# Moving an encoder layer's SBUF tiles: one pool for each kind of tile, and one residue for all that TensorE reads

## Chip, cores, metric

The kernel runs on one core of one Trainium2 chip. The metric is the device time of one execution in microseconds, as the median of several runs.

## What is computed

One layer of an encoder trunk on 2048 tokens of width 1024, all in float32: adaptive scale, shift and gate from a conditioning vector `c`, a stick-breaking attention with 16 heads, and a SwiGLU feed-forward (width 2816), each between two RMS norms. Cut to what matters:

```python
def stick_breaking_mixer(h, w_qkv, w_o):
    ...
    for q0 in range(0, s, SB_BLOCK):                 # 128 queries at a time
        z = einsum('bthd,bshd->bhts', q[:, q0:end], k[:, :end]) * scale
        mask = s_pos < t_pos
        sp = where(mask, softplus(z), 0.0)
        rest = cumsum(sp, axis=3, reverse=True)
        a = exp(where(mask, z - rest, -inf))
        outs.append(einsum('bhts,bshd->bthd', a, v[:, :end]))
    return concatenate(outs, axis=1).reshape(b, s, D_MODEL) @ w_o

def swiglu_ffn(h, w_in, w_out):
    g, u = split(h @ w_in, 2, axis=-1)
    return (silu(g) * u) @ w_out

h = modulate(rms_norm(x, norm_g[i, 0]), sh_m, sc_m)
x = x + gt_m * rms_norm(stick_breaking_mixer(h, ...), norm_g[i, 1])
h = modulate(rms_norm(x, norm_g[i, 2]), sh_f, sc_f)
x = x + gt_f * rms_norm(swiglu_ffn(h, ...), norm_g[i, 3])
```

## The kernel before

A float32 product is made of three passes in the fp32r format: each operand is split into a rounded high part (ScalarE) and the remainder (VectorE or GpSimd), and `mm3` (L146 to L150) multiplies high by high (L148), high by low (L149) and low by high (L150). Nearly all matmuls have a moving operand of 128 x 512 and a stationary one of 128 x 128; every one brings its own weight load (PEld in the profile).

The order of work is written out by hand and fixed for all engines but SyncE, which issues the DMAs. Four stages follow one another.

- **Attention** (to about 1430 us). Eight pairs of heads, four blocks of 512 tokens. Projections (`pj`, moving `ht`, stationary `w`) run in threes between the slots of the attention: in a slot, two matmuls make the scores (`z`, L507: moving `kt`, stationary `qt`), ScalarE takes two sigmoids, VectorE a running product (`tensor_tensor_scan`, L536 and L541), GpSimd a product (L548), TensorE turns the result by matmuls with the identity (`t`, L558: the identity is the moving operand, the turned tile `a` the stationary one; 2176 of them), ScalarE and VectorE split it (`aT`), and two matmuls weigh the values (`o`, L586: moving `aT`, stationary `v`). Another 384 transposes turn the input, the values and the second norm's rows, 128 each.
- **Output projection** (`y`: moving `wo`, stationary `ohl`), to about 1580 us: 32 tiles of 24 matmuls.
- **First FFN product** (`s`: moving `r`, stationary `l`), to about 2444 us, by a scheme with seven products in the place of eight. 44 column groups of 84 matmuls each: products 1, 5, 6, 3, 7, 2, 4, four blocks of the contraction in each, three passes in each block. The right factors `r` stay in SBUF over 22 groups, in buffers of the kinds that `RIGHT_TAGS` names: `kt` for the first 9 matmuls of a group, then `v` for 9, `qt` for 18, `kt` for 12, `v` for 12, `whl` for 24. The left factors `l` are in `ht` buffers.
- **Second FFN product** (`o` of `b`, `ol`), to the end: 56 steps of 33 matmuls, moving `b` (in `kt` and `v` buffers, seven in turn of each), stationary `ol_qt` for the first 24 matmuls of a step (`qt` buffers) and `ol_aT` for the last 9 (`aT` buffers).

SBUF tiles are named by a tag, and each tag has a fixed number of buffers (`BUFS`, L51). Before, all tags lie in one pool, `att` (L153), which sets them down in the order in which they first appear, small tiles among large ones. In the built program this gives the following places (byte address in a partition, and the address modulo 512, which the parts of a tile share, since they start at multiples of 512):

| kind | bytes x buffers | address before | modulo 512 | address after | modulo 512 |
|---|---|---|---|---|---|
| identity (in `begin`) | 512 | 2,688 | 128 | 3,136 | 64 |
| `qt` | 8192 x 3 | 4,160 | 64 | 45,632 | 64 |
| `v` | 4096 x 7 | 28,736 | 64 | 70,208 | 64 |
| `wraw`, `qkn` | 4096 x 2 each | 57,408, 65,600 | 64 | 176,704, 184,896 | 64 |
| `ht` | 8192 x 5 | 73,792 | 64 | 4,672 | 64 |
| `a` | 2048 x 10 | 114,752 | 64 | 201,280 | 64 |
| `w` (scan results) | 2052 x 3 | 135,232 | 64, 96, 128 | 221,760 | 64, 96, 128 |
| `kt` | 4096 x 7 | 141,472 | 160 | 98,880 | 64 |
| `whl` | 8192 x 4 | 170,752 | 256 | 127,552 | 64 |
| `tmp` | 2048 x 4 | 203,520 | 256 | 193,088 | 64 |
| `aT` | 4096 x 4 | 211,712 | 256 | 160,320 | 64 |
| single columns | 4 to 32 | 170,144 and 228,096 | many | 228,000 | many |

Of the kernel before, what the change touches and what calls it, by code (L numbers as in the profile page):

```python
# [9 lines left out]
F32 = mybir.dt.float32  # L10
# [6 lines left out]
P = 128  # L17
# [61 lines left out]
    return ap.bitcast(F32)  # L79


@with_exitstack
def hybrid_trunk_kernel(
    ctx: ExitStack,
# [14 lines left out]
    nc = tc.nc  # L99

    const = ctx.enter_context(tc.tile_pool(name="const", bufs=1))
    dram = ctx.enter_context(tc.tile_pool(name="dram", bufs=1, space=DRAM))


    begin = const.tile([P, BT + 1], F32, name="begin")
    nc.gpsimd.memset(begin, 0.0)
    ident = begin[:, BT - P : BT]
# [42 lines left out]
        nc.tensor.matmul(acc, lhs[1], rhs[0], start=False, stop=last, **kw)  # L150


    att = ctx.enter_context(tc.tile_pool(name="att", bufs=2))  # L153
    zps = ctx.enter_context(tc.tile_pool(name="zps", bufs=3, space=PSUM))
    tps = ctx.enter_context(tc.tile_pool(name="tps", bufs=2, space=PSUM))
    accps = ctx.enter_context(tc.tile_pool(name="accps", bufs=3, space=PSUM))
# [1224 lines left out]
    for n, (s, f) in enumerate(groups):  # L1381
# [3 lines left out]
        for at, product in enumerate(PRODUCTS):  # L1385
            acc = banks_of[{1: 0, 6: 0, 7: 0, 4: 0, 5: 1, 3: 1, 2: 2}[product]]
            for k in range(H4):
# [18 lines left out]
                if s == 0 and 4 <= f < 4 + 2 * H4:  # L1406
                    kt, second = divmod(f - 4, 2)
# [177 lines left out]
```

## Time and profile before

| | us |
|---|---|
| median of 3 runs | 2883.05 |
| lowest, highest | 2881.68, 2887.14 |
| span of the profiled execution, its own time | 2881.7 |

The span runs from the first to the last instruction, and equals the fastest of the three runs to a tenth. Times in the profile are counted from its start. A matmul's recorded duration (some 390 ns for 512 columns) overlaps those of its neighbours, since matmuls are pipelined: the pace is the distance from one start to the next. The lines themselves stand with the prediction.

### The profile page before, as it was taken

How to read it: one execution, taken by the hardware profiler on the slowest of the kernel's cores; microseconds unless marked ns; L12 is line 12 of the kernel's file. 1: busy time of each engine (PE TensorE's matmuls, PEld its weight loads, DVE VectorE, ACT ScalarE, POOL GpSimd, SP SyncE). 2: the span in 40 equal slices, each digit the busy share in tenths (PEclk: the TensorE clock that was granted, in tenths of full speed). 3: DMA queues.
4: the chain of work that ended last, by engine and by line, in shares of the span. 5: the costliest groups of instructions: out<-in, count | busy, mean ns of one | idle time of the engine just before them, and what ended most of it. 6: DMA issues, size and time to landing. Idle time of an engine off the chain costs nothing.

```text
span 2881.7 us, 41790 instructions
## 1 busy us (share of the span) xinstructions
PE 2836.6 (98%) x13848; PEld 2337.5 (81%) x13848; DVE 2029.2 (70%) x2823; ACT 1630.5 (57%) x3263; POOL 1280.0 (44%) x2032
## 2 busy tenths in 40 slices
PE   8999999999999999999999999999999999999998
PEld 6788888888888888887888788888778888888887
DVE  6788888888888888889866766555775555133477
ACT  4787777787777877778645533334433334322343
POOL 1475666566576655657310122222122222544454
PEclk9999999999999999999999999999999999999999
DMA  8764546656665644555388544334363234544565
GB/s 313 279 207 166 187 155 222 208 178 221 196 213 174 214 125 161 190 158 200 119 286 317 170 147 153 106 110 165 110 193 106 93 110 161 190 141 149 176 220 184
DMA packets 239368, 516.84 MB, mean 179 GB/s; under 512 B 22320, under 2 KB 110384, under 8 KB 221488
## 3 DMA queue, kind: packets, MB, share of 16 engines
q1 hardware_dynamic: 239152, 514.18, 54.1%
q8 instruction: 109, 1.79, 0.2%
q14 instruction: 107, 0.88, 0.1%
HBM read 346.85 MB, written 118.49 MB: 161 GB/s over the span
## 4 chain that ended last, share of the span: by engine, by line
PE 91%; DVE 4%; DMA 2%; ACT 2%; issue 1%; POOL 0%; SPq 0%; DVEq 0%; POOLq 0%; ACTq 0%
PE s L148 9%; PE s L149 9%; PE s L150 9%; PE o L586 8%; PE z L507 8%; PE t L558 8%; PE pj L148 6%; PE pj L150 6%; PE pj L149 6%; PE o L149 5%; PE o L150 5%; PE o L148 5%; PE y L148 2%; PE y L150 2%; PE y L149 2%
## 5 line engine op out<-in xcount | busy, mean ns | idle before, releaser
L548 POOL TENSOR_TENSOR a<-a,w 128x512 f32<-128x512 f32 (+3 forms) x640 | 619.7, 968 | 221.4 <-DVE w L541 127.8
L541 DVE TENSOR_TENSOR_SCAN w<-z,c,begin 128x512 f32<-128x512 f32 x384 | 489.7, 1279 | 87.2 <-ACT z L526 66.9
L148 PE MATMUL s<-r,l 128*128 128x512 f32 x1232 | 486.1, 395 | 3.0 <-DVE p L1348 3.0
L149 PE MATMUL s<-r,l 128*128 128x512 f32 x1232 | 484.3, 393 | 0.0
L150 PE MATMUL s<-r,l 128*128 128x512 f32 x1232 | 483.7, 393 | 0.0
L524 ACT ACTIVATE a<-z 128x512 f32<-128x512 f32 (+3 forms) x640 | 346.9, 542 | 172.1 <-PE z L507 135.2
L586 PE MATMUL o<-aT,v 128*128 128x512 f32 (+3 forms) x1280 | 387.3, 384 | 0.1
L574 DVE TENSOR_TENSOR aT<-t,aT 128x512 fp32r<-128x512 f32 (+3 forms) x640 | 359.3, 595 | 23.1 <-ACT aT L568 22.6
L507 PE MATMUL z<-kt,qt 128*128 128x512 f32 (+3 forms) x1280 | 364.8, 366 | 0.0
L568 ACT CAST aT<-t 128x512 fp32r<-128x512 f32 (+3 forms) x640 | 313.9, 533 | 74.9 <-PE t L558 64.5
L526 ACT ACTIVATE z<-z 128x512 f32<-128x512 f32 (+3 forms) x640 | 345.5, 540 | 0.0
L1356 POOL TENSOR_TENSOR one<-p,p 128x512 f32<-128x512 f32 x44 | 71.2, 1617 | 590.5 <-issue 326.8
L148 PE MATMUL pj<-ht,w 128*128 128x512 f32 x768 | 312.5, 407 | 5.7 <-DVE qn L411 1.4
L149 PE MATMUL pj<-ht,w 128*128 128x512 f32 x768 | 304.2, 396 | 1.1 <-DVE ht L321 0.5
L150 PE MATMUL pj<-ht,w 128*128 128x512 f32 x768 | 304.5, 397 | 0.0
L558 PEld LDWEIGHTS t<-begin,a 128*128 128x128 f32 x2176 | 255.6, 141 | 58.8 <-DVE aT L574 10.9
L558 PE MATMUL t<-begin,a 128*128 128x128 f32 x2176 | 294.7, 273 | 8.5 <-DVE aT L574 7.4
L148 PEld LDWEIGHTS s<-r,l 128*128 128x128 f32 x1232 | 231.2, 188 | 58.5 <-ACT l L1209 2.3
L150 PEld LDWEIGHTS s<-r,l 128*128 128x128 f32 x1232 | 231.1, 188 | 53.8
L149 PEld LDWEIGHTS s<-r,l 128*128 128x128 f32 x1232 | 231.1, 188 | 53.3 <-issue 0.5
L507 PEld LDWEIGHTS z<-kt,qt 128*128 128x128 f32 x1280 | 230.2, 188 | 40.2 <-DVE w L536 0.2
L536 DVE TENSOR_TENSOR_SCAN w<-z,begin 128x128 f32<-128x128 f32 (+3 forms) x256 | 208.7, 818 | 75.6 <-ACT z L526 64.3
(158 smaller groups left out, 4879.7 us busy)
## 6 DMA issues: line engine op xcount, KB each, us to landing
ht<-h_s SPq DMA_DIRECT2D x108, 1024.0 KB, 8.1
wi<-in_win SPq DMA_DIRECT2D x86, 512.0 KB, 4.0
qt<-qn SPq DMA_DIRECT2D x124, 256.0 KB, 4.8
ol_qt<-act_s SPq DMA_DIRECT2D x56, 512.0 KB, 3.6
act_s<-S SPq DMA_DIRECT2D x66, 256.0 KB, 4.1
br<-in_wout SPq DMA_DIRECT2D x66, 256.0 KB, 3.5
h_s<-ht SPq DMA_DIRECT2D x16, 1024.0 KB, 8.0
o_s<-os SPq DMA_DIRECT2D x128, 128.0 KB, 2.6
```

What stands on the lines that cost most here:

```text
L148: nc.tensor.matmul(acc, lhs[0], rhs[0], start=first, stop=False, **kw)
L149: nc.tensor.matmul(acc, lhs[0], rhs[1], start=False, stop=False, **kw)
L150: nc.tensor.matmul(acc, lhs[1], rhs[0], start=False, stop=last, **kw)
L507: nc.tensor.matmul(z[:, :n], q[:, e, part, r * P : (r + 1) * P], k[:, e, :n], start=part == 0, stop=part == 1,)
L524: nc.scalar.activation(a[:, :n], z[:, :n], AF.Sigmoid, scale=QK_SCALE)
L526: nc.scalar.activation(z[:, :n], z[:, :n], AF.Sigmoid, scale=-QK_SCALE)
L541: nc.vector.tensor_tensor_scan(rest[:, rev], left[:, rev], begin[:, :BT][:, rev], initial=carries[r], op0=ALU.mult, op1=ALU.bypass,)
L548: nc.gpsimd.tensor_tensor(a[:, :n], a[:, :n], rest[:, 1 : n + 1], op=ALU.mult)
L558: nc.tensor.transpose(pt[:, rb * P : (rb + 1) * P], weighed[i, rb][:, j * P : (j + 1) * P], ident)
L568: nc.scalar.copy(hl[:, 0, t0:], pt[:, t0:])
L574: nc.vector.tensor_tensor(hl[:, 1, t0:], pt[:, t0:], f32(hl[:, 0, t0:]), op=ALU.subtract)
L586: nc.tensor.matmul(acc[:, t0:], lhs, hl[:, part, t0:], start=sc == qb and j == 0 and part == 0, stop=sc == 0 and j == 3 and part == 1,)
```

## The change

The one pool `att` is replaced by an object with the same `tile` method that has a pool of its own for each large kind, opened in the order of `PLACES`, and a last pool `rest` for all others: the three `w` buffers, and all single columns. Two fillers shift what follows: `lead`, 448 bytes ahead of `begin`, brings the identity to residue 64, and `gap_ht`, 64 bytes ahead of `ht`, brings all large kinds there (their sizes are multiples of 512). Each filler is set to zero once by VectorE. Sizes, buffer counts, tags and all other code stay as they are. In the built program every engine has the same instructions in the same order on the same tiles, with the same waits, but for the two added `memset`s on VectorE; the table above has the addresses.

```diff
+PLACES = [("ht", 64), ("qt", 0), ("v", 0), ("kt", 0), ("whl", 0), ("aT", 0), ("wraw", 0), ("qkn", 0), ("tmp", 0), ("a", 0)]
+
+
+class Places:
+
+    def __init__(self, ctx, tc):
+        self.of = {}
+        for tag, gap in PLACES:
+            if gap:
+                pool = ctx.enter_context(tc.tile_pool(name=f"gap_{tag}", bufs=1))
+                self.of[f"gap_{tag}"] = pool
+                tc.nc.vector.memset(pool.tile([P, gap // 4], F32, name=f"gap_{tag}"), 0.0)
+            self.of[tag] = ctx.enter_context(tc.tile_pool(name=f"at_{tag}", bufs=1))
+        self.rest = ctx.enter_context(tc.tile_pool(name="rest", bufs=1))
+
+    def tile(self, shape, dtype, name, tag, bufs):
+        return self.of.get(tag, self.rest).tile(shape, dtype, name=name, tag=tag, bufs=bufs)
...
+    lead = const.tile([P, 112], F32, name="lead")
+    nc.vector.memset(lead, 0.0)
     begin = const.tile([P, BT + 1], F32, name="begin")
...
-    att = ctx.enter_context(tc.tile_pool(name="att", bufs=2))
+    att = Places(ctx, tc)
```

## The prediction

> **What bounds the kernel now.** I read the page first: busy shares, granted clock, and the chain that ended last.
>
> ```profile
> span 2881.7 us, 41790 instructions
> PE 2836.6 (98%) x13848; PEld 2337.5 (81%) x13848; DVE 2029.2 (70%) x2823; ACT 1630.5 (57%) x3263; POOL 1280.0 (44%) x2032
> ...
> PEclk9999999999999999999999999999999999999999
> ...
> PE 91%; DVE 4%; DMA 2%; ACT 2%; issue 1%; POOL 0%; SPq 0%; DVEq 0%; POOLq 0%; ACTq 0%
> ```
>
> TensorE is the bound: 98% busy, 91% of the chain, at full clock. So I asked whether that holds in each stage (table by stage: stretch, its length, busy us of PE, PEld, DVE, ACT, POOL, then clock, DMA share, GB/s).
>
> ```profile
> 700.00:1000.00 300.00, 295.71 (x1627) 249.43 (x1626) 257.07 (x340) 234.59 (x495) 195.54 (x392) 1.00 0.60 193
> 1430.00:1580.00 150.00, 148.87 (x692) 120.80 (x691) 101.43 (x209) 75.59 (x171) 16.02 (x25) 1.00 0.86 303
> 2010.00:2444.00 434.00, 431.72 (x1863) 349.08 (x1862) 277.00 (x368) 160.77 (x287) 107.32 (x69) 1.00 0.41 132
> 2444.00:2870.00 426.00, 426.00 (x1840) 345.36 (x1839) 191.22 (x268) 143.72 (x248) 212.81 (x131) 1.00 0.55 177
> ```
>
> The longest line of TensorE's waits (total us, times, longest):
>
> ```profile
> PE t L558 <- DVE aT L574: 7.4, 14, 1.2
> ```
>
> From 1430 us on (output projection, both FFN products) TensorE has no wait to speak of, and VectorE is at about two thirds or less. In the attention VectorE stands at 257 of 300 us, 86%, behind TensorE's 296; the longest of TensorE's waits is 7.4 us in all. So what matters is how long one matmul takes, and the change touches only where its operands lie: each engine gets the same instructions in the same order, with the same waits, but for two small memsets on VectorE. Buffer counts stay too, so no transfer starts under another condition.
>
> **Does the place set a matmul's pace? The trace already has the comparison.** Matmuls are pipelined, so their pace is the distance from start to start. One column group of the first FFN product is 84 matmuls, in this order of the moving tile's place (residue modulo 512, from the table of places): 9 at 160 (kt), 27 at 64 (v, then qt), 12 at 160 (kt), 12 at 64 (v), 24 at 256 (whl). The stationary tile (ht) is at 64 throughout. The timeline of one group, TensorE alone; I keep the rows at which the place changes, and the one at which the pace settles (columns: start, duration):
>
> ```profile
> 1701.78 0.39 PE L148 MATMUL s<-r,l 128*128 128x512 f32 x1
> ...
> 1703.88 0.39 PE L148 MATMUL s<-r,l 128*128 128x512 f32 x1
> ...
> 1705.27 0.39 PE L148 MATMUL s<-r,l 128*128 128x512 f32 x1
> ...
> 1710.03 0.40 PE L148 MATMUL s<-r,l 128*128 128x512 f32 x1
> ...
> 1712.84 0.40 PE L148 MATMUL s<-r,l 128*128 128x512 f32 x1
> ...
> 1714.92 0.39 PE L148 MATMUL s<-r,l 128*128 128x512 f32 x1
> ...
> 1715.60 0.39 PE L148 MATMUL s<-r,l 128*128 128x512 f32 x1
> ...
> 1721.20 0.39 PE L148 MATMUL s<-r,l 128*128 128x512 f32 x1
> ```
>
> Differences over counts: kt, (1703.88-1701.78)/9 = 233 ns; v, the first 6, 1.39/6 = 232; then v and qt, 4.76/21 = **227**; kt, 2.81/12 = 234; v, the first 9, 2.08/9 = 231; the last 3, 0.68/3 = 227; whl, 5.60/24 = **233**. So with moving and stationary tile both at 64 the pace settles at 227 ns, after six to nine matmuls in which an earlier change of place is still felt; with the moving tile elsewhere it stays at 233 to 234. The second FFN product, with other tiles and other code, shows the same: v with qt, kt with qt, then kt with aT, which is at 256:
>
> ```profile
> 2600.15 0.39 PE L148 MATMUL o<-b,ol_qt 128*128 128x512 f32 x1
> ...
> 2601.51 0.40 PE L148 MATMUL o<-b,ol_qt 128*128 128x512 f32 x1
> ...
> 2602.92 0.39 PE L148 MATMUL o<-b,ol_aT 128*128 128x512 f32 x1
> ...
> 2605.02 0.39 PE L148 MATMUL o<-b,ol_qt 128*128 128x512 f32 x1
> ```
>
> 1.36/6 = 227 ns with both at 64, 1.41/6 = 235, 2.10/9 = 233. The Trainium skill speaks against the change here. "SBUF — State Buffer", under "Who interferes with whom", says that PE never waits on anyone, and "TensorE: Matmul & The Clock Gate", under "Step-by-step", that loading the next weights takes no read bandwidth from the running matmul; by these the change gives nothing. The trace differs by 6 ns a matmul. I go by the trace, and keep the rule as a rival.
>
> **The sum.** After the change every operand named above, and the identity of the transposes, is at 64, so I take 227 ns (226.7 from 4.76/21) for each 512-column matmul.
> - First FFN product: a group takes 1721.20-1701.78 = 19.42 us now and 84 x 0.2267 = 19.04 then: 0.38 us, in 44 groups **16.7 us**.
> - Second FFN product, 56 steps of 33 matmuls:
>
> ```profile
> L148 PE MATMUL o<-b,ol_qt x448: 387/392/399, 2444.2 to 2869.7; 128*128 128x512 f32 x150
> ...
> L150 PE MATMUL o<-b,ol_aT x168: 388/393/400, 2450.3 to 2872.3; 128*128 128x512 f32 x168
> ```
>
> From 2444.2 to 2872.3 it is 1847 distances, 428.1 us, 231.8 ns each; at 226.7 they are 418.7 us: **9.4 us**.
> - In the stages with transposes between, distances are mixed, so I use the recorded duration, which moves with them: 389 ns in the settled stretch above (1705.2 to 1710.0 us), 394 in the last 24 of the group (1715.55 to 1721.15). Groups by form in those two stretches (busy us, mean ns):
>
> ```profile
> L148 PE MATMUL s<-r,l 128*128 128x512 f32 x7 | 2.7, 389 | 0.0
> ...
> L148 PE MATMUL s<-r,l 128*128 128x512 f32 x8 | 3.2, 394 | 0.0
> ```
>
> The other products by line (minimum/median/maximum ns):
>
> ```profile
> L149 PE MATMUL y<-wo,ohl x256: 387/394/400, 1346.2 to 1579.9; 128*128 128x512 f32 x128
> ...
> L149 PE MATMUL pj<-ht,w x768: 387/394/796, 21.6 to 1336.0; 128*128 128x512 f32 x192
> ```
>
> And by form over the whole run:
>
> ```profile
> L507 PE MATMUL z<-kt,qt 128*128 128x512 f32 x896 | 283.6, 397 | 0.0
> ...
> L586 PE MATMUL o<-aT,v 128*128 128x512 f32 x896 | 301.9, 418 | 0.1
> ```
>
> Output projection: 3 lines x 256 x 5 ns = **3.8 us**. Attention: projections 3 x 768 x 5 = 11.5; scores 896 x 6 = 5.4 (397 is a mean with some waits in it, so I count 6 of the 8); weighted values 896 x 5 = 4.5 (the 418 has the start-up after the transposes in it, which I leave). That is 21.4 us if TensorE alone decides there. VectorE at 86% and waits of a few us say that it mostly does; where a slot waits on a scan, the gain turns into a longer wait. I take three quarters: **16 us**, between 0 and 21.
> - The 2176 transposes, and 384 like them:
>
> ```profile
> L558 PEld LDWEIGHTS t<-begin,a x2176: 137/141/146, 106.1 to 1417.9; 128*128 128x128 f32 x198
> L558 PE MATMUL t<-begin,a x2176: 270/272/332, 106.3 to 1418.0; 128*128 128x128 f32 x198
> ```
>
> and eight of them in the timeline:
>
> ```profile
> 299.95 1.03 PE L558 MATMUL t<-begin,a 128*128 128x128 f32 x8
> ```
>
> They take 1.03 us, the last one's 272 ns included: (1030-272)/7 = 108 ns each, identity at 128, turned tile at 64. No row shows both at 64. By the matmul rows it should not be slower; I count nothing, with 2 ns either way for the range, 5 us in all.
> - The other engines' operands move as well. ScalarE's rounding of the left factor reads from 256 in one form (ls) and from 64 in the other (wi), and takes the same:
>
> ```profile
> L1209 ACT CAST l<-ls 128x512 fp32r<-128x512 f32 x172 | 106.1, 618 | 6.5 <-DVE ls L1192 6.5
> ...
> L1209 ACT CAST l<-wi 128x512 fp32r<-128x512 f32 x129 | 79.0, 613 | 35.3 <-ACT l L1209 32.6 <-issue 1.7 <-PE s L150 0.9
> ```
>
> So nothing there. If a faster TensorE frees buffers 1.6% sooner, DMA at 41 to 60% in the long stages has room.
> - The two memsets run at the head of VectorE's queue, before the first sums:
>
> ```profile
> 0.84 0.17 DVE L110 MEMSET ones<- 128x128 f32 x1 [0.84 <-PEq L1572]
> ...
> 6.42 0.49 DVE L627 TENSOR_SCALAR asum<-ac,c_act 128x512 f32<-128x512 f32 x1 [5.34 <-DMA ac<-in_ada_first]
> ```
>
> They are smaller than the 0.17 us one, so under 0.35 us together; queued behind them are two memsets and the sums, and those wait 5.34 us for the first weights anyway. Without that cover they would cost 0.35 us once.
>
> 16.7 + 9.4 + 3.8 + 16 = 46 us. The profiled execution took its span of 2881.7 us, the fastest of the three runs (2881.68); the median, 2883.05, is 1.4 above. I forecast the median: 2883 - 46 = **2837 us**; this case's own range is 2824 (all 21 us of the attention, 5 from the transposes, and some 3 from start-ups after transposes) to 2846.
>
> **Rivals.**
> *The attention does not settle.* There the runs of equal matmuls are short: three of a projection, two of a score, then transposes. The FFN needed six to nine matmuls to settle after a change of place; if a change of form does the same, the attention keeps its 394 ns and the gain is 16.7 + 9.4 + 3.8 = 30: 2853 us. Against: the minimum in those groups is 387 already, with places mixed. Chance 0.08.
>
> *It is the height in memory, not the residue.* Every slow tile (kt, whl, aT) lies above 141,000 bytes before, every fast one below 115,000. After, kt comes down to 98,880 to 127,552, while whl and aT stay above 127,552. Then only what reads kt gains: scores 5.4 us; of the FFN group's 0.38 us all but whl's 24 x 6.6 ns = 0.16, so 0.22 x 44 = 9.7; in the second product about half of the 1344 matmuls with qt, 670 x (235-227) = 5.4; some 1.5 of the output projection's 3.8. 22 us: 2861. For: before, the two are never apart. Against: a tile at 64 that follows kt is slow for a while although it is itself low, which a phase explains and a height doesn't. Chance 0.06.
>
> *The change does nothing for the pace*, as the skill's pages would have it, and the 227 belongs to those products for another reason: 2883. Against: the pace follows the tile within one group, and in two stages with different code. Chance 0.07.
>
> *Slower: the transposes collide.* Identity and turned tile come to the same residue for the first time, and in a transpose both are 128 columns wide, so that the load of the next tile and the stream of the identity could meet on every step. There are 2176 + 384 = 2560; the gain is lost from 46/2560 = 18 ns each on (126 instead of 108). If each then took a whole weight load of 141 ns, with none of it beside another, it is 2560 x 33 = 84 us, less 46: 38 us slower, 2921. Against: 512-column matmuls with both at 64 are the fastest here. Chance 0.05.
>
> **How the numbers follow.** Forecast 0.74, rivals 0.08, 0.06, 0.07, 0.05. The range goes from the forecast's low end, 2824, up past the first two rivals to 2866; left out are the last two, 0.12, and tails. A measurement of this kernel tells 0.2% from no change, so faster are the first three, 0.88; same 0.07; slower 0.05.
>
> **What would show it.** In the profile after: a group of 84 in 19.04 us with no step at its kt and whl tiles; medians of 389 in the FFN and near it in the attention; transposes at 108; ScalarE and VectorE durations unchanged; VectorE's share in the attention a point up. Wrong: 394 still at aT and whl (height), 394 in the attention alone (no settling), more than 1.03 us for eight transposes (collision), or TensorE's waits in the attention up by over 10 us.

## The result and the profile after

The change takes 2849.16 us (median of 4 runs, 2849.01 to 2854.84) against 2882.81 (2881.68 to 2887.14): a ratio of 0.9887, 95% interval 0.9873 to 0.9901, 33.65 us less. The forecast was 46. The profiled execution after has a span of 2846.9 us and a time of 2849.01, so a time is about 2.1 us above its span; span to span the gain is 34.8 us.

The page after, busy shares and the chain that ended last:

```profile
span 2846.9 us, 41792 instructions
...
PE 2797.7 (98%) x13848; PEld 2333.6 (82%) x13848; DVE 2031.8 (71%) x2825; ACT 1629.6 (57%) x3263; POOL 1278.3 (45%) x2032
...
PE 88%; DVE 5%; issue 2%; ACT 2%; DMA 1%; POOL 1%; SPq 0%; DVEq 0%; POOLq 0%; ACTq 0%
```

TensorE still fills 98% of the span and still makes most of the chain. Its busy time fell by 38.9 us with the same 13,848 matmuls; that of VectorE, ScalarE and GpSimd moved by 2.6 us at most. So the matmuls became shorter, nothing else did.

One column group of the first FFN product, from the timeline of TensorE after (start, duration). The rows are the first of each kind of tile, as in the group shown of before: kt, v and qt, kt, v, whl, and the next group:

```profile
1688.48 0.39 PE L169 MATMUL s<-r,l 128*128 128x512 f32 x1
...
1690.52 0.39 PE L169 MATMUL s<-r,l 128*128 128x512 f32 x1
...
1696.64 0.39 PE L169 MATMUL s<-r,l 128*128 128x512 f32 x1
...
1699.36 0.39 PE L169 MATMUL s<-r,l 128*128 128x512 f32 x1
...
1702.08 0.39 PE L169 MATMUL s<-r,l 128*128 128x512 f32 x1
...
1707.52 0.39 PE L169 MATMUL s<-r,l 128*128 128x512 f32 x1
```

2.04/9, 6.12/27, 2.72/12, 2.72/12 and 5.44/24 are all 227 ns. The steps at kt and whl are gone and the group takes 19.04 us, the forecast value to two decimals.

The lines of mm3 and of the transposes after (minimum/median/maximum ns, first and last start):

```profile
L169 PE MATMUL s<-r,l x1232: 389/389/798, 1568.5 to 2417.1; 128*128 128x512 f32 x176
...
L169 PE MATMUL o<-b,ol_qt x448: 387/389/396, 2417.7 to 2836.0; 128*128 128x512 f32 x150
...
L170 PE MATMUL pj<-ht,w x768: 387/390/792, 21.6 to 1326.5; 128*128 128x512 f32 x192
...
L169 PE MATMUL y<-wo,ohl x256: 387/389/481, 1336.4 to 1567.9; 128*128 128x512 f32 x128
...
L171 PE MATMUL pj<-ht,w x768: 387/393/628, 22.2 to 1326.7; 128*128 128x512 f32 x192
...
L171 PE MATMUL y<-wo,ohl x256: 389/389/496, 1336.9 to 1568.3; 128*128 128x512 f32 x128
...
L171 PE MATMUL o<-b,ol_aT x168: 388/389/389, 2423.6 to 2838.5; 128*128 128x512 f32 x168
...
L579 PE MATMUL t<-begin,a x2176: 270/272/330, 104.4 to 1407.6; 128*128 128x128 f32 x198
```

From the second stage on every median is 389. In the projections it is 389, 390 and 393 by line: the attention did not settle fully. The transposes are as before (272), and eight of them still take 1.03 us, at 800.62 in the timeline:

```profile
800.62 1.03 PE L579 MATMUL t<-begin,a 128*128 128x128 f32 x8
```

The two lines of before whose first starts the table needs beside those shown with the prediction:

```profile
L148 PE MATMUL s<-r,l x1232: 387/394/799, 1580.4 to 2443.5; 128*128 128x512 f32 x176
...
L148 PE MATMUL y<-wo,ohl x256: 387/394/486, 1346.0 to 1579.7; 128*128 128x512 f32 x128
```

By the first and last starts of these lines, the 34.8 us come from the stretches below. A stretch ends where the next product's first matmul starts, so the attention's last turns (transposes, to 1418.0 us before and 1407.6 after) lie in the output projection's stretch:

| stretch | before | after | gained | forecast |
|---|---|---|---|---|
| start to the first transpose | 106.3 | 104.4 | 1.9 | 0 |
| attention, to the first `y` | 1239.7 | 1232.0 | 7.7 | 16 |
| output projection | 234.4 | 232.1 | 2.3 | 3.8 |
| first FFN product | 863.8 | 849.2 | 14.6 | 16.7 |
| second FFN product | 428.1 | 420.8 | 7.3 | 9.4 |
| tail | 9.4 | 8.4 | 1.0 | 0 |

### The profile page after: what moved, and what is told of

It reads as the page before. It is cut to its first block, busy times and chain, and to the rows that moved or that the text cites. A ratio compares the mean times of both kernels' runs of the same rounds, so it can differ in the third digit from the quotient of the medians.

```text
span 2846.9 us, 41792 instructions
## 1 busy us (share of the span) xinstructions
PE 2797.7 (98%) x13848; PEld 2333.6 (82%) x13848; DVE 2031.8 (71%) x2825; ACT 1629.6 (57%) x3263; POOL 1278.3 (45%) x2032
## 4 chain that ended last, share of the span: by engine, by line
PE 88%; DVE 5%; issue 2%; ACT 2%; DMA 1%; POOL 1%; SPq 0%; DVEq 0%; POOLq 0%; ACTq 0%
PE s L169 9%; PE s L171 9%; PE s L170 9%; PE z L528 8%; PE o L607 8%; PE t L579 8%; PE pj L169 6%; PE pj L170 6%; PE pj L171 6%; PE o L171 5%; PE o L169 5%; PE o L170 5%; PE y L171 1%; PE y L169 1%; PE y L170 1%
```

## The experiments

Each kernel is the change with the edit shown, and runs beside the kernel before. A number in `PLACES` is the gap in bytes ahead of a tag, and moves all that follow. Theories: the residue sets the pace (which equality, modulo what, is open); the height in memory does; the pools or the small tiles at the end do; the transposes hold part of the gain.

**1. The heights of before, at the residue of after**, so that kt, whl and aT lie above 135,000 bytes again.

```diff
-PLACES = [("ht", 64), ("qt", 0), ("v", 0), ("kt", 0), ("whl", 0), ("aT", 0), ("wraw", 0), ("qkn", 0), ("tmp", 0), ("a", 0)]
+PLACES = [('qt', 64), ('v', 0), ('wraw', 0), ('qkn', 0), ('ht', 0), ('a', 0), ('kt', 0), ('whl', 0), ('tmp', 0), ('aT', 0)]
```

> The pools of the change, in another order, so that kt, whl, tmp and aT lie as high as before (135,744; 164,416; 197,184; 205,376) and v, qt, ht as low, but all at residue 64, the identity too. Theory (the residue decides): the same as the change, 2849 us within 3, first FFN product settled at 227 ns at every tile. Rival (the height decides): kt, whl and aT are slow again, 233 ns in the FFN, about 2880 us.

2849.23 us (2848.94 to 2850.04), ratio 0.9883 (0.9868 to 0.9898): all of the gain is kept. The height does nothing.

**2. The residues of before, in the new pools**: kt at 160, whl, aT and tmp at 256, the identity at 128, small tiles still at the end.

```diff
+PLACES = [('ht', 0), ('qt', 0), ('v', 0), ('wraw', 0), ('qkn', 0), ('a', 0), ('kt', 96), ('whl', 96), ('aT', 0), ('tmp', 0)]
...
-    lead = const.tile([P, 112], F32, name="lead")
-    nc.vector.memset(lead, 0.0)
```

> A pool for each kind as in the change, small tiles at the end, but the residues of before: identity 128, kt 160, whl, aT and tmp 256, the rest 64. Theory: the pools and the small tiles do nothing by themselves, so the time of before, 2883 us within 3. Rival (grouping the tiles or moving the small ones is what helps): nearer to 2849 than to 2883.

2882.03 us (2880.47 to 2886.6, 10 runs), ratio 0.9999 (0.9989 to 1.0008): all of the gain is gone. Its first FFN product by line:

```profile
L167 PE MATMUL s<-r,l x1232: 387/394/799, 1577.4 to 2442.2; 128*128 128x512 f32 x176
```

394 again. With the first run this settles the cause: pools, order and small tiles do nothing; the residue does it all.

**3. The identity alone back at 128.**

```diff
+PLACES = [('ht', 0), ('qt', 0), ('v', 0), ('kt', 0), ('whl', 0), ('aT', 0), ('wraw', 0), ('qkn', 0), ('tmp', 0), ('a', 0)]
...
-    lead = const.tile([P, 112], F32, name="lead")
-    nc.vector.memset(lead, 0.0)
```

> The change without the filler ahead of the identity: the identity at 128, all else at 64. Theory: transposes are paced by their weight loads at 108 ns, and the identity's place is felt at most in how far matmuls behind the transposes are from settling: 2849 us, up to 5 more. FFN unchanged. Rival (the identity carries a part of the gain): 2856 us or more, with the loss in the attention only.

2852.95 us (2849.99 to 2855.57), ratio 0.9895 (0.988 to 0.991). The distances of the attention are those of the change (means of those between 222 and 246 ns: projections 229.79 against 229.74, scores 231.11 against 231.09). The profiled execution's first transpose starts at 109.0 us in place of 104.4, and from there to the first `y` it takes 1232.5 us against 1232.0: 4.6 of the 6.5 us that its span has more lie in the start, where its granted clock stood at 0.52 from 91.9 to 95.3 us. No effect of the identity's place on the pace is visible.

**4. All at residue 0 in place of 64.**

```diff
-    lead = const.tile([P, 112], F32, name="lead")
+    lead = const.tile([P, 96], F32, name="lead")
...
+PLACES = [('ht', 64), ('qt', 0), ('v', 0), ('kt', 0), ('whl', 0), ('aT', 0), ('wraw', 0), ('qkn', 0), ('tmp', 0), ('a', 0)]
```

> Everything that the change puts at 64 is put at residue 0. Theory (equal residues of the moving and the stationary tile decide, not which residue): 2849 us within 3, FFN at 227 ns. Rival (64 is a good place by itself, as 256, also a multiple of 64, was a bad one): FFN at about 233 ns and 2875 us or more.

2851.39 us (2848.63 to 2856.17), ratio 0.9891 (0.9875 to 0.9908). 64 is not special: both operands at 0 do as well.

**5 and 6. A sweep of differences**, one execution each. In the first, `ht` (stationary) stays at 64 and the moving tiles of the first FFN product come to 96 (v), 128 (kt), 192 (qt) and 320 (whl). In the second the differences are negative: `ht` 320, v 288, kt 256, whl 224, qt 192.

```diff
+PLACES = [('ht', 0), ('aT', 0), ('wraw', 0), ('qkn', 0), ('tmp', 0), ('a', 0), ('v', 32), ('kt', 32), ('qt', 64), ('whl', 128)]
```
```diff
+PLACES = [('aT', 0), ('wraw', 0), ('qkn', 0), ('tmp', 0), ('a', 0), ('qt', 128), ('whl', 32), ('kt', 32), ('v', 32), ('ht', 32)]
```

> The kinds at different residues, with ht, aT, a and the raw tiles at 64 and the identity at 128: v at 96, kt at 128, qt at 192, whl at 320. In the first FFN product the stationary tile (ht) is then 32, 64, 128 and 256 bytes below the moving one, by stretches. Theory (equal modulo 512 is needed): every stretch settles at 231 to 237 ns, about 2880 us in all. Rival (a shorter period, 128 bytes, is what counts; 192 and 96, which were slow, are no multiples of it): the qt and whl stretches run at 227, v and kt not.

> The same with the stationary tile above the moving one: ht at 320, v at 288, kt at 256, whl at 224, qt at 192, the rest at 64. Theory (equal modulo 512): no stretch at 227, about 2880 us. Rival (period of 128): the qt stretch at 227. Rival (only the order counts, a stationary tile behind the moving one is free): all stretches at 227 or less.

2877.4 and 2885.49 us. In the second, no stretch settles at 227: differences of -32, -64, -96 and -128 all run at 232 to 234 on average. In the first, +32 and +128 run at about 233 and +64 at 229, but the stretch on whl, 256 above its stationary tile, comes to 227. Its rows in the timeline (the first of whl, the one from which it is settled, the first of the next group):

```profile
1709.81 0.39 PE L167 MATMUL s<-r,l 128*128 128x512 f32 x1
...
1711.19 0.39 PE L167 MATMUL s<-r,l 128*128 128x512 f32 x1
...
1715.27 0.40 PE L167 MATMUL s<-r,l 128*128 128x512 f32 x1
```

1.38/6 = 230 ns, then 4.08/18 = 227. That was not expected: the places need not be equal modulo 512, a difference of 256 will do. A period of 128 falls, since +128 and -128 are slow.

One thing in the first sweep goes the other way. Its scores have the moving `kt` at 128 and the stationary `qt` at 192, and their mean distance (of those between 222 and 246 ns) is 229.64 ns, against 231.09 in the change with both at 64. In runs of a few matmuls, equal places are not the quickest that was seen; why is open, since what runs just before the scores has other places too.

**7. 256 tried on the whole kernel**: kt, whl and aT at 320, all else at 64.

```diff
+PLACES = [('ht', 64), ('qt', 0), ('v', 0), ('wraw', 0), ('qkn', 0), ('tmp', 0), ('a', 0), ('kt', 256), ('whl', 0), ('aT', 0)]
```

> The change, but kt, whl and aT at 320 and all others, the identity too, at 64, so that in the projections, the scores, the weighted values, and most of both FFN products one operand is at 64 and the other at 320, and they are equal modulo 256 but not modulo 512. After the whl stretch of the sweep, which ran at 227 ns with 256 between, the theory is: equal modulo 256 is enough, 2849 us within 4, FFN at 227 everywhere. Rival (equal modulo 512 is needed, and the stretch of the sweep was a special case): about 2880 us.

2849.61 us (2848.82 to 2851.66), ratio 0.9881 (0.9864 to 0.9897): the same as the change. Equal modulo 256 is enough.

**8. One kind back: `whl` at 256**, all else at 64.

```diff
+PLACES = [('ht', 64), ('qt', 0), ('v', 0), ('kt', 0), ('aT', 0), ('wraw', 0), ('qkn', 0), ('tmp', 0), ('a', 0), ('whl', 192)]
```

> The change, but whl alone at 256 again. Theory: in the first FFN product the 24 matmuls on whl take 6.6 ns more, 24 x 6.6 x 44 = 7.0 us, and the first six to nine on kt behind them some 4 ns more, 1.3 us; in the output projection, whose whl tiles are half of the moving ones with gaps, some 1.5 us, in the attention (stationary tile of the projections) up to 4: 2861 us, 2857 to 2864. Rival (a single kind out of place disturbs all, since the phase never settles): 2868 us or more.

2859.39 us (2859.1 to 2862.19), ratio 0.9917 (0.9902 to 0.9931), 10.2 us above the change. The first FFN product takes 857.7 us instead of 849.2: 8.5 us. Place by place in the group, the 24 on `whl` stand at 233.3 ns in place of 226.9, 6.8 us over the 44 groups, and the nine on `kt` behind them, of which the first five are not settled, at 228.9 in place of 226.8, another 0.8. What is left of the 8.5 is no matter of places: in this execution the granted clock stood at 0.53 from 2018.4 to 2021.8 us, where eight distances in a row were 413 to 427 ns, some 1.6 us more in all, partly made up by shorter waits elsewhere. The rest of the 10.2 is in the attention (1.6 us; projections, with weights in `whl`, 229.74 to 230.91 ns) and the output projection (0.7). So in the FFN a kind in the wrong place costs what its matmuls' count says; the 2304 projections of the attention lose only 1.2 ns each.

**9. Where the attention's missing part is: one turn in each slot**, in place of two in every second one (the list that orders a slot's steps), so that TensorE changes between forms oftener with the same matmuls.

```diff
-    [("av", 9), ("score", 0), ("proj", 0), ("turn", 6), ("turn", 5),
...
+    [("av", 9), ("score", 0), ("proj", 0), ("turn", 6),
+     ("sig", 0), ("stick", 0), ("high", 6), ("low", 6)],
+    [("av", 9), ("score", 0), ("proj", 0), ("turn", 6),
...
-    [("av", 9), ("score", 0), ("proj", 0), ("high", 6), ("low", 6), ("sig", 0), ("stick", 0)],
```

> The change, but the two turns of four transposes that stood together in every second slot of the attention stand apart, one in each slot, so that there are 320 more changes between transposes and 512-column matmuls, with the same work. Theory (after transposes the pace must settle again, six to nine matmuls long at 231 to 236 ns, and that is what the attention still loses): medians of the attention's matmuls back at about 394, and 320 x (6 + 7 x 3) ns = 9 us slower than the change, 2858 us, 5 to 15. Rival (the attention is held back by the other engines): no slower than 2852.

2858.74 us (2856.84 to 2858.91), ratio 0.991 (0.9894 to 0.9927): 9.6 us above the change. The scores' median goes from 389 to 393, and so does the pace (scores 231.09 to 233.18 ns, weighted values 228.82 to 230.93, projections 229.74 to 230.64):

```profile
L529 PE MATMUL z<-kt,qt x1280: 220/393/522, 87.7 to 1400.5; 128*128 128x512 f32 x128, 128*128 128x384 f32 x19, 128*128 128x128 f32 x18, 128*128 128x256 f32 x18
```

By the pace, over some 2300 projections and 900 each of the other two, this is about 6 us. The start-up behind transposes adds some: the groups of transposes go from 320 to 640, and a change from a transpose to a 512-column matmul takes 28 + 314 ns where settled steps of the two kinds would take 109 + 227, 6 ns more. By stretches, the attention takes 1239.3 us in place of 1232.0, so 7.3 of the 9.3 us between the two spans; another 2.3 lie ahead of the first transpose (106.7 against 104.4 us), with the granted clock at 0.51 for 6.8 us, as in run 10 (106.8 us), which lacks this edit. So the 9 us expected for the attention were 7.3, and that the times differ by 9.6 is in part luck. The medians did not come as expected either: the projections stay at 390 and 393, not about 394.

**10. The turned tiles alone at 192.**

```diff
+PLACES = [('ht', 64), ('qt', 0), ('v', 0), ('kt', 0), ('whl', 0), ('aT', 0), ('wraw', 0), ('qkn', 0), ('tmp', 0), ('a', 128)]
```

> The change, but the tiles that the transposes turn (a) at 192, with the identity and all else at 64: the stationary operand of the transposes alone is out of place, by 128. Theory: a transpose is paced by its weight load, so 108 ns as before; the pace behind it must settle in any case, so the attention keeps its pace and the time is 2849 us within 4. Rival (how far the pace behind the transposes is from settled hangs on the places in them): medians in the attention and the matmuls behind the transposes of the output projection move, by up to 10 us either way.

2851.72 us (2850.21 to 2852.98), ratio 0.9886 (0.9872 to 0.9901), with the pace of the attention's matmuls as in the change (projections 229.63, scores 231.10). At the places tried, a transpose's two operands matter neither by themselves nor for what follows.

No version beat the change by more than its spread.

## Why the prediction came out as it did

**Right: the place sets the pace, by the residue.** Runs 1 and 2 take the two apart, and the height rival falls. The rival that nothing happens falls with the 33 us: by the rules of the Trainium skill, as the prediction read them ("SBUF — State Buffer", "Who interferes with whom"; "TensorE: Matmul & The Clock Gate", "Step-by-step"), run 2 and the change would take the same, and they are 2882.03 and 2849.16. What the prediction put too narrowly is the condition. "Both at 64" is the case it had; equal modulo 256, at 0, at 64, or at 64 with 320, is what the runs show.

**Right: transposes, other engines, memsets.** Transposes keep 108 ns in pace, so the collision rival falls. ScalarE's rounding after, now from one place in both forms, against 618 and 613 before (busy us, mean ns):

```profile
L1230 ACT CAST l<-ls 128x512 fp32r<-128x512 f32 x172 | 106.2, 618 | 7.0 <-DVE ls L1213 7.0
L1230 ACT CAST l<-wi 128x512 fp32r<-128x512 f32 x129 | 79.1, 614 | 32.3 <-ACT l L1230 29.8 <-issue 1.7 <-PE s L171 0.9
```

The two memsets, 0.15 and 0.07 us, end before 1.2 us, and VectorE then waits 5.17 us for the first weights, as told (timeline of VectorE after):

```profile
0.83 0.15 DVE L125 MEMSET lead<- 128x112 f32 x1 [0.83 <-PEq L1593]
...
1.08 0.07 DVE L93 MEMSET gap_ht<- 128x16 f32 x1
...
6.39 0.49 DVE L648 TENSOR_SCALAR asum<-ac,c_act 128x512 f32<-128x512 f32 x1 [5.17 <-DMA ac<-in_ada_first]
```

**Wrong in size: the attention, 16 us for 7.7.** The prediction took three quarters of 21.4 because a slot that waits on a scan would turn the gain into a longer wait. That is not what happened. The longest of TensorE's waits after:

```profile
PE t L579 <- DVE aT L595: 7.2, 14, 1.2
```

7.2 us against 7.4: it did not grow, and VectorE's busy time in 700 to 1000 us went from 257.07 only to 257.93, 0.3 points of share where one was expected. What failed is the 5 to 6 ns a matmul. The by-form rows after, where the prediction read 397 and 418:

```profile
L528 PE MATMUL z<-kt,qt 128*128 128x512 f32 x896 | 281.8, 396 | 0.0
...
L607 PE MATMUL o<-aT,v 128*128 128x512 f32 x896 | 299.0, 415 | 0.1
```

They fell by 1 and 3 ns. Means of the distances between 222 and 246 ns, before and after: projections 231.36 to 229.74, scores 232.94 to 231.09, weighted values 232.27 to 228.82; settled is 226.7. So a matmul gained 1.6, 1.9 and 3.5 ns, and over some 2150, 851 and 652 distances in that range this is 7.3 us, nearly all of the stretch's 7.7. The part above 226.7 that is left there is 6.6, 3.8 and 1.4 us. So the rival "the attention does not settle" was half the truth, at a chance of 0.08: the pace settles neither not at all nor fully. The output projection shows how, since in part of it four transposes come after every nine matmuls. Timeline of TensorE after (the first `y` row is the second matmul behind the transposes):

```profile
1455.74 0.60 PE L916 MATMUL h2T<-begin,x1n 128*128 128x128 f32 x4
...
1456.41 0.40 PE L170 MATMUL y<-wo,ohl 128*128 128x512 f32 x1
...
1458.49 0.39 PE L170 MATMUL y<-wo,ohl 128*128 128x512 f32 x1
...
1460.99 0.39 PE L169 MATMUL y<-wo,ohl 128*128 128x512 f32 x1
```

Behind the transposes, nine distances of 2.08/9 = 231 ns, then 2.50/11 = 227. Every operand here is at 64; a change of form does what a change of place did in the FFN. The attention's rows after, from 110 to 1336 us, say the same when its distances are sorted by their place in a run of 512-column matmuls (a run ends at a transpose or a shorter matmul): the first ten average 230.28 ns, all later ones 226.67. Before, the two are 231.67 and 231.89. Only 440 of the 2780 distances in range are later ones, so little of the attention is settled, and all that it has left above the settled pace lies in the first ten. The same walk shaved the output projection to 2.3 of 3.8 us. Run 9, with twice as many groups of transposes, has no run of over ten matmuls and moves the same way. Why the pace walks at all stays open.

The trace of before could have sized this: the v stretches needed six to nine matmuls, and 471 of the attention's 568 runs have at most ten. The prediction had the first number and knew that the runs are short, put both in the rival, and priced the forecast as if settled.

**Wrong in size: the two FFN products, by about 2 us each.** The pace came in as forecast (19.04 us, 389 ns), and part was given back in waits, which the prediction had as "no wait to speak of". TensorE's waits after, from 1560 us on:

```profile
PE s L169 <- DVE p L1369: 3.9, 3, 2.5
PE o L171 <- POOL ol_qt L1262: 1.5, 2, 1.1
```

The first was 3.0 us before. In all, the first product's distances over 246 ns, which are such waits and the start-ups behind them, add 1.5 us. The second wait, for GpSimd's split of the left factors, was not there: TensorE now gets to two of them first, and two distances of the second product grow to 0.76 and 1.50 us. This part varies: with equal places the second product took 419.2 to 420.1 us in the profiles of runs 1, 3, 4, 7 and 10, against 420.8 here.

**Wrong: the time of the execution.** The span was taken as the time itself, which it undercuts by 2.1 us; the profiled execution before took some 2883.8 us by that, an estimate, and is none of the runs listed. This did not move the forecast, since that subtracts from the median. The 1.9 us at the start and the 1.0 at the end are not in the sum. The start is no gain of the pace: the first transpose, at 106.3 us before and 104.4 after, starts at 109.0 in run 3 and 106.8 in run 10. It goes with the granted clock of the one execution. The same stretch before and after (busy us and counts of the engines, clock, DMA share, GB/s):

```profile
29.40:36.20 6.80, 6.80 (x19) 5.36 (x19) 6.28 (x14) 2.70 (x4) 0.00 (x0) 0.50 1.01 413
```
```profile
29.40:36.20 6.80, 6.03 (x35) 4.69 (x36) 6.54 (x14) 2.70 (x4) 0.00 (x0) 1.00 1.02 414
```

At a clock of 0.50 TensorE did 19 matmuls there, at 1.00 it did 35. The tail is no gain either: it is 8.3 us in run 2, which has the residues of before.

The sum by its terms: 46 forecast; 8.3 less in the attention, 1.5 in the output projection, 4.2 in the FFN products, makes 31.9; with 2.9 from start and tail, 34.8 from span to span. The time, 2849.16, lies 3 us above the case's own range, which ended at 2846. That it lies inside the range given is owed to the room kept there for the first two rivals, and in that sense it is luck: the mechanism was right in the FFN, and the sum was over a third too large.

## What to carry to other kernels

Where TensorE bounds a kernel of back-to-back 512-column matmuls in fp32r, put the moving and stationary tiles of each product at equal addresses modulo 256 bytes; in long runs of equal matmuls a kind that is off costs some 6 to 8 ns for each of its matmuls here (233.3 or 234.5 ns against 226.8 in the FFN), whatever its pool or height. Only differences that are multiples of 32 bytes were tried, in fp32r alone. Look for the difference in one trace first: compare start-to-start distances of the same line across kinds of tile, because means hide it. Price the gain only for the part of a run of equal matmuls that lies behind the settling, five to ten matmuls here.

## What the runs showed of the hardware that was not expected

- The condition has a period of 256 bytes: a difference of 256 runs at 227 ns and the whole kernel at 2849.61 us; differences of 32, 96, 128 and 192 (whl before) run at 232 to 234, one of +64 at 229, one of -64 at 233.
- After a change of place or of form, the pace walks for five to ten matmuls, at 224 to 236 ns in turn in the FFN, before it stays at 227: six and eight at the changes to v before, five at the change back to 64 behind whl in run 8, nine behind transposes in the output projection, up to ten in the attention.
- Transposes (128 columns, identity moving) show no such dependence: 108 ns with identity and turned tile at 64 and 64, 128 and 64, or 64 and 192.
- In short runs an unequal place can be quicker: scores with kt at 128 and qt at 192 at 229.64 ns, both at 64 at 231.09.
- What lies behind the 256 bytes and behind the walk stays open: no run here shows it.
